# Both attentions of a two-layer decoder: softmax weights turned and copied once in full precision, and multiplied with V head by head onto two halves of the output rows

## The chip, the cores and the metric

The kernel runs on one core of one Trainium2 chip. A core has a matrix engine (TensorE, PE in the rows; its weight loads are listed apart as PEld), a vector engine (VectorE, DVE), a scalar engine (ScalarE, ACT), a general engine (GpSimd, POOL) and DMA queues, issued here by SyncE (SP) and by GpSimd. The metric is the device time of one execution in microseconds (us); lower is better. Every engine runs its own instructions in the order in which the program has them, and waits for the others through semaphores.

## The reference, cut to what matters

Two layers over 1024 tokens with 16 heads of 64 in 4 groups. Layer A ("NSA") has three attention branches per head, over compressed blocks, selected blocks and a window of 256. Each branch is a softmax that is normalised and gated, and the three are added:

```
q, kc, vc, ks, vs, kwn, vwn, gl = split(rmsnorm(x) @ w_in)
p_cmp = softmax(q @ k_cmp.T + bias)              # 63 compressed blocks
p_sel = softmax(q @ ks.T + bias, chosen blocks)  # up to 1024 keys
p_win = softmax(q @ kwn.T + bias, 256 keys)
o = g0 * (p_cmp @ v_cmp) + g1 * (p_sel @ vs) + g2 * (p_win @ vwn)
x = x + o @ w_out ;  x = x + swiglu(rmsnorm(x))
```

Layer B has three dilated windows per head over shared K and V; each gives an output and a log-sum-exp, and the three are merged by their denominators. After it come an output projection, a SwiGLU and a final norm. In both layers the step that matters here is `p @ v`: softmax weights of 128 queries times V of 64 columns, for each head.

## The kernel before, in words

Stages follow each other on the core: projections of layer A, attention A (`cmp_job`, `dense_job`), a dense stage (output projection, SwiGLU, projections for B), attention B (`wide_job`, `near_job`, which share `unit`), and the last dense stage. The instruction order on each engine is fixed when the program is built; the functions below only say what is issued.

An attention job works on 128 queries and a pair of heads (hp is 0 or 1, e is the head within the pair; four heads of a group share one V). Its front makes scores on TensorE (L790 and L791 in A, L1672, L1677 and L1692 in B, always two products each, because queries and keys are held as a high and a low part), adds the bias and takes the extreme on DVE (L793, L1638), and takes the exponential on ACT (L799, L1643); in A POOL scales (L803). Its back, two jobs later, turns the weights `P`, 128 x 128 at a time, on TensorE into a bank `pt` (`transposed`, L328), brings them to SBUF, and multiplies with V into the bank `o`.

The high and low parts are how the kernel gets accuracy out of TensorE's faster product for the type float32r ("fp32r"): `split` makes the high part with an ACT copy (`th`, L165) and the low part with a DVE subtraction (`tl`, L166). A V tile holds 128 columns for each key: 64 of the high part and 64 of the low part. So one product of V (128 columns, as the weight) with 256 columns of turned weights (both heads of a pair for one block of 128 keys) gives 128 output rows, of which the upper 64 must be added to the lower 64. `mm_pv` does this once with `th` (L348) and once with `tl` (L349). Where `whole` is set, one full-precision copy (L332) and one plain float32 product (L347) take their place. For some blocks `copy` is given: ACT or DVE copies (L340), and POOL makes both parts (L341, L342). `evac_o` adds the two halves of the rows: ACT copies one half (L359), DVE adds the other (L360).

In the compressed branch each of the four heads has its own 128-column tile (64 used, 64 zero) in `pc`; four are turned, and two products of 512 columns with `vc` (L760, L761) begin the bank `o`.

Of the kernel before, what the change touches and what calls it, by code (L numbers as in the profile page):

```python
# [10 lines left out]
F32 = mybir.dt.float32  # L11
# [13 lines left out]
G = 4  # L25
# [90 lines left out]
def trunk(ctx, tc, I, out):  # L116
# [206 lines left out]
    def transposed(p, blocks, copy=None, bufs=4, whole=False):  # L323


        ps = bank("pt")
        for i, b in enumerate(blocks):
            nc.tensor.transpose(ps[:, i * 128:(i + 1) * 128], b, ident)  # L328
        w = len(blocks) * 128
        if whole:  # L330
            tf = p.tile([128, 512], F32, name="traw", bufs=2)
            nc.scalar.copy(tf[:, :w], ps[:, :w])  # L332
            return tf, None
# [11 lines left out]
    def mm_pv(o_, v, th, tl, cs, first, last):  # L345
        if tl is None:
            return nc.tensor.matmul(o_, f32(v), th[:, cs], start=first, stop=last, skip_group_check=True)  # L347
        nc.tensor.matmul(o_, v, th[:, cs], start=first, stop=False, skip_group_check=True)  # L348
        return nc.tensor.matmul(o_, v, tl[:, cs], start=False, stop=last, skip_group_check=True)  # L349

    cp_a, cp_v = nc.scalar.copy, nc.vector.tensor_copy

    def evac_o(p, po, dst):

        ov = po[:].rearrange("p (c e q) -> p c e q", e=2, q=128)
        tmp = p.tile([128, 2, 128], F32, name="ot", bufs=2)
        for e in range(2):
            own, oth = slice(64 * e, 64 * e + 64), slice(64 - 64 * e, 128 - 64 * e)
            nc.scalar.activation(tmp[own], ov[oth, :, e, :], AF.Copy)  # L359
            nc.vector.tensor_add(dst[own], ov[own, :, e, :], tmp[own])  # L360
# [20 lines left out]
    vS = dram.tile([2, NT, 128, G, 128], F32, name="vS")  # L381
# [8 lines left out]
    vc = ares.tile([128, G, 128], F32R, name="vc")  # L390
# [4 lines left out]
    with ExitStack() as c:  # L395
# [51 lines left out]
        def evac_v(i):  # L447
            def f(t, ps):
                vt = st.tile([128, G, 128], F32R, name="vt", bufs=2)
# [44 lines left out]
        def compress(i, kc2, weights):  # L494
# [35 lines left out]
            else:  # L530
                for g in range(G):
                    for hd in range(2):
                        nc.tensor.matmul(ps2[0:64, g * 64:(g + 1) * 64], hid[:, hd, g * 64:(g + 1) * 64],
                                         w2t[:, hd, 0, :], start=hd == 0, stop=hd == 1)
                nc.scalar.activation(vc[64:128], kc2[64:128, :, 0:128], AF.Copy, scale=0.0)
                split(vc[0:64, :, 0:64], vc[0:64, :, 64:128], ps2[0:64].rearrange("p (g d) -> p g d", d=64))
# [87 lines left out]
    with ExitStack() as c:  # L624
# [9 lines left out]
        rVs = Ring("V", [128, 4, 128], F32R, [(kA1, 2), (kB, 1)])  # L634
        rVw = [Ring(f"VW{i}", [128, 4, 128], F32R, [((kA0, kA1)[i], 1)]) for i in range(2)]
# [55 lines left out]
        def load_v(i, g, a):  # L691
            t_ = grp["V", i, g, a] = (rVs if i == 0 else rVw[a]).tile()
            nc.sync.dma_start(f32(t_), vS[i, 4 * a:4 * a + 4, :, g, :].rearrange("t p d -> p t d"))

        pcs = [wk.tile([128, 4, 128], F32, name=f"pc{i}") for i in range(2)]
        for pc in pcs:
            nc.gpsimd.memset(pc[:, :, 64:], 0.0)
# [8 lines left out]
        def cmp_job(g, t):  # L706
# [50 lines left out]
            def back():  # L757
                th, tl = transposed(wk, [pc[:, hh, :] for hh in range(4)])
                po = po_[g, t] = bank("o")
                nc.tensor.matmul(po, vc[:, g, :], th, start=True, stop=False, skip_group_check=True)  # L760
                nc.tensor.matmul(po, vc[:, g, :], tl, start=False, stop=False, skip_group_check=True)  # L761
            return back

        def dense_job(g, t, br, hp):
# [41 lines left out]
            def back():  # L806
                po = po_[g, t]
                for b0 in range(0, nb, 2):
                    bs = range(b0, min(b0 + 2, nb))
                    th, tl = transposed(wk, [P[:, e, b * 128:(b + 1) * 128] for b in bs for e in range(2)],  # L810
                                        (cp_a, cp_v)[hp] if br == 2 and b0 == 2 else None,
                                        whole=br == 2 and hp == 1 and b0 == 0)
                    for i, b in enumerate(bs):
                        last = br == 1 and b == nb - 1
                        cs = slice(i * 256, (i + 1) * 256)
                        o_ = po[:, hp * 256:(hp + 1) * 256]
                        v_ = grp["V", br - 1, g, (k0 + b) // 4][:, (k0 + b) % 4, :]
                        mm_pv(o_, v_, th, tl, cs, False, last)
# [1025 lines left out]
```

## Time and profile before

| | us |
|---|---|
| median of 3 runs | 2938.28 (2936.68 to 2944.49) |
| the profiled execution | 2938.84, of which the span from first to last instruction is 2937.1 |
| attention A | 280 to 717 of the span |
| attention B | 1856 to 2178 of the span |
| TensorE busy over the span | 2816.6 (96%) |
| DVE, ACT, POOL busy | 2398.0 (82%), 1621.1 (55%), 1642.7 (56%) |

The busy time of TensorE counts each product from its start to a modelled end, and products overlap at their ends; so what an instruction costs in a stream is the distance from the end of the one before to its own end, which is called its slot below. The granted TensorE clock is 0.989 of full (2.4 GHz) over the span.

### The profile page before, as it was taken

The numbers are of one execution on the slowest core, as the hardware profiler recorded it, in microseconds if no ns is written. First come the engines' busy times: TensorE is split into PE (matmuls) and PEld (weight loads), VectorE is DVE, ScalarE is ACT, GpSimd is POOL, SyncE is SP. The second block draws the span as 40 slices with busy tenths as digits, with TensorE's granted clock in tenths as the row PEclk, the third lists the DMA queues.
The fourth block names the chain that finished last, engine by engine and source line by source line (L and its number), as shares of the span: only waits on it lengthen the run. The fifth ranks groups of instructions, "written<-read, shape, count | busy, mean of one in ns | idle before, by whom it ended". The sixth has DMA issues, their size and how long they took to land. (4 is left out here: it accounts for less than half of the span.)

```text
span 2937.1 us, 44584 instructions
## 1 busy us (share of the span) xinstructions
PE 2816.6 (96%) x14734; PEld 2375.5 (81%) x14734; DVE 2398.0 (82%) x4866; ACT 1621.1 (55%) x3615; POOL 1642.7 (56%) x1727
## 2 busy tenths in 40 slices
PE   9999999999999999999999999899989999999997
PEld 8888888887778888888777778788867788888886
DVE  5543988988888989989976777699998788888887
ACT  5432988887563433334454444699975543343334
POOL 3135766765566556556547777444425655666562
PEclk9999999999999999999999999999999999999999
DMA  8678132112322222231225555865431211112112
GB/s 255 212 240 296 34 105 82 44 47 80 108 62 65 71 73 69 62 85 52 84 85 153 155 162 148 278 201 164 136 136 52 69 57 59 58 47 65 54 44 76
DMA packets 277319, 317.59 MB, mean 108 GB/s; under 512 B 19196, under 2 KB 210733, under 8 KB 277088
## 3 DMA queue, kind: packets, MB, share of 16 engines
q1 hardware_dynamic: 255344, 246.50, 27.8%
q0 software_dynamic: 21744, 68.23, 7.4%
q8 instruction: 117, 1.92, 0.3%
q14 instruction: 114, 0.93, 0.1%
HBM read 243.17 MB, written 87.20 MB: 112 GB/s over the span
## 5 line engine op out<-in xcount | busy, mean ns | idle before, releaser
L885 DVE TENSOR_TENSOR pl<-oT,ph 128x512 fp32r<-128x512 f32 x337 | 350.8, 1058 | 57.5 <-PE dr L934 17.4
L884 ACT ACTIVATE ph<-oT 128x512 fp32r<-128x512 f32 x347 | 210.9, 626 | 203.7 <-PE ux L1082 54.6
L328 PE MATMUL pt<-ident,P 128*128 128x128 f32 x1536 | 243.7, 276 | 11.0 <-DVE tl L166 5.3
L166 DVE TENSOR_TENSOR tl<-pt,th 128x512 fp32r<-128x512 f32 (+1 forms) x336 | 217.5, 653 | 27.2 <-ACT th L165 25.7
L884 ACT ACTIVATE ph<-oTb 128x512 fp32r<-128x512 f32 x239 | 145.6, 627 | 170.4 <-PE ux L1082 52.9
L885 DVE TENSOR_TENSOR pl<-oTb,ph 128x512 fp32r<-128x512 f32 x233 | 213.2, 937 | 28.9 <-PE dr L934 17.4
L939 DVE TENSOR_TENSOR xr<-xr,dr 128x512 f32<-128x512 f32 x320 | 204.0, 679 | 15.9 <-PE dr L934 15.4
L803 POOL TENSOR_SCALAR P<-P,sm,gates 128x384 f32<-128x384 f32 (+7 forms) x256 | 183.4, 728 | 44.8 <-DVE sm L801 39.7
L939 DVE TENSOR_TENSOR xr<-xr,dx 128x512 f32<-128x512 f32 x320 | 204.6, 678 | 1.9 <-PE dx L934 1.9
L165 ACT ACTIVATE th<-pt 128x512 fp32r<-128x512 f32 (+1 forms) x336 | 185.6, 565 | 35.6 <-PE pt L328 31.0
L328 PEld LDWEIGHTS pt<-ident,P 128*128 128x128 f32 x1536 | 178.7, 141 | 32.0 <-DVE tl L166 5.3
L1266 POOL TENSOR_TENSOR oT<-oT,gffn 128x512 f32<-128x512 f32 x92 | 113.5, 1244 | 139.7 <-DMA oT<-in_ffn_w_up_dram 101.8
L799 ACT ACTIVATE P<-P,m 128x384 f32<-128x384 f32 (+7 forms) x256 | 170.7, 669 | 9.0 <-DVE m L797 7.2
L1266 POOL TENSOR_TENSOR oTb<-oTb,gffn 128x512 f32<-128x512 f32 x92 | 109.7, 1199 | 99.6 <-DMA oTb<-in_ffn_w_up_dram 69.1
L349 PE MATMUL o<-tl,V 128*128 128x256 f32 x572 | 159.1, 300 | 6.4 <-POOL tl L342 2.8
L348 PE MATMUL o<-th,V 128*128 128x256 f32 x572 | 159.8, 298 | 3.7 <-DVE o L360 2.2
L341 POOL TENSOR_SCALAR th<-traw 128x256 fp32r<-128x256 f32 x112 | 95.7, 854 | 105.9 <-DVE traw L340 40.2
L1643 ACT ACTIVATE P<-P,st 128x384 f32<-128x384 f32 (+2 forms) x256 | 139.7, 548 | 7.7 <-DVE st L1638 6.4
L1638 DVE CUSTOM_DVE_ANT_0 P<-s,T 128x384 f32<-128x384 f32 (+2 forms) x256 | 114.8, 476 | 12.8 <-PE s L1677 4.6
L349 PEld LDWEIGHTS o<-tl,V 128*128 128x128 f32 x572 | 108.6, 190 | 16.5 <-DVE tl L166 11.0
L348 PEld LDWEIGHTS o<-th,V 128*128 128x128 f32 x572 | 108.9, 190 | 12.4 <-DVE o L360 5.3
L884 ACT ACTIVATE ph<-wd 128x512 fp32r<-128x512 f32 x86 | 53.6, 627 | 99.8 <-PE ux L1082 48.5
(642 smaller groups left out, 9096.1 us busy)
## 6 DMA issues: line engine op xcount, KB each, us to landing
qB<-xr POOLq DMA_DIRECT2D x96, 256.0 KB, 4.6
oT<-in_ffn_w_up_dram SPq DMA_DIRECT2D x92, 256.0 KB, 2.9
oTb<-in_ffn_w_up_dram SPq DMA_DIRECT2D x92, 256.0 KB, 2.9
Q<-qB SPq DMA_DIRECT2D x40, 512.0 KB, 5.8
wd<-in_ffn_w_down_dram SPq DMA_DIRECT2D x66, 256.0 KB, 2.5
oT<-in_b_w_q_dram SPq DMA_DIRECT2D x48, 256.0 KB, 4.5
K<-kBs SPq DMA_DIRECT2D x40, 256.0 KB, 8.6
wraw<-in_a_w_in_dram SPq DMA_DIRECT2D x18, 512.0 KB, 7.4
```

The lines of the kernel that those rows point to most:

```text
L165: prev = nc.scalar.activation(H_, src, AF.Copy)
L166: rest = (eng or nc.vector).tensor_sub(L_, src, f32(H_))
L328: nc.tensor.transpose(ps[:, i * 128:(i + 1) * 128], b, ident)
L348: nc.tensor.matmul(o_, v, th[:, cs], start=first, stop=False, skip_group_check=True)
L349: return nc.tensor.matmul(o_, v, tl[:, cs], start=False, stop=last, skip_group_check=True)
L799: nc.scalar.activation(P[:, e, :n], P[:, e, :n], AF.Exp, bias=mm[:, e:e + 1], scale=-1.0, accum_out=sm[:, e:e + 1])
L803: nc.gpsimd.tensor_scalar(P[:, e, :n], P[:, e, :n], sm[:, e:e + 1], gt(g, t, br, 2 * hp + e, 1), op0=OP.mult, op1=OP.mult)
L884: nc.scalar.activation(h, src, AF.Copy)
L885: (eng or nc.vector).tensor_sub(l, src, f32(h))
L939: nc.vector.tensor_add(xs, xs, banks[t])
L1266: nc.gpsimd.tensor_mul(v, v, gains[:, k:k + 4].unsqueeze(2).to_broadcast([128, 4, 128]))
L1643: nc.scalar.activation(P[:, e, :n], P[:, e, :n], AF.Exp, bias=stats[:, slot, hh:hh + 1], scale=-1.0, accum_out=stats[:, slot, 4 + hh:5 + hh])
```

## The change

The turned weights are copied once to SBUF as float32 (`turned_heads`, tile `pT`), by ACT or by DVE in turn. V and the compressed V are kept as plain float32 with 64 columns for each key. `pv_heads` multiplies V with each head's 128 columns apart: head e of the pair writes output rows 64e to 64e + 63, so that the bank `o` ends with both heads below each other, and one DVE copy takes it to the output. The compressed blocks' weights of two heads (64 + 64 columns) are turned together, against a `vc` that holds V_cmp twice, on the diagonal of a 128 x 128 block. The tiles of V in DRAM and SBUF are half as large.

```diff
-    def transposed(p, blocks, copy=None, bufs=4, whole=False):
-        ...
-        th = p.tile([128, 512], F32R, name="th", bufs=bufs)
-        tl = p.tile([128, 512], F32R, name="tl", bufs=bufs)
-        if copy is None:
-            split(th[:, :w], tl[:, :w], ps[:, :w])
-        else:
-            raw = p.tile([128, 512], F32, name="traw", bufs=2)
-            copy(raw[:, :w], ps[:, :w])
-            nc.gpsimd.tensor_scalar(th[:, :w], raw[:, :w], 1.0, None, op0=OP.mult)
-            nc.gpsimd.tensor_sub(tl[:, :w], raw[:, :w], f32(th[:, :w]))
-        return th, tl
+    def turned_heads(p, blocks, copy):
+        ps = bank("pt")
+        for i, b in enumerate(blocks):
+            nc.tensor.transpose(ps[:, i * 128:(i + 1) * 128], b, ident)
+        w = len(blocks) * 128
+        t = p.tile([128, 512], F32, name="pT", bufs=5)
+        copy(t[:, :w], ps[:, :w])
+        return t
+
+    def pv_heads(po, hp, v, pT, first, last):
+        for e in range(2):
+            prev = nc.tensor.matmul(po[64 * e:64 * e + 64, hp * 128:(hp + 1) * 128], v, pT[:, e * 128:(e + 1) * 128],
+                                    start=first, stop=last, skip_group_check=True)
+        return prev
...
-    vS = dram.tile([2, NT, 128, G, 128], F32, name="vS")
+    vS = dram.tile([2, NT, 128, G, DH], F32, name="vS")
...
-                split(vt[:, :, 0:64], vt[:, :, 64:128], ps[:, :256].rearrange("p (g d) -> p g d", d=64))
-                nc.gpsimd.dma_start(vS[i, t], f32(vt))
+                nc.scalar.copy(vt, ps[:, :256].rearrange("p (g d) -> p g d", d=DH))
+                nc.gpsimd.dma_start(vS[i, t], vt)
...
-                nc.scalar.activation(vc[64:128], kc2[64:128, :, 0:128], AF.Copy, scale=0.0)
-                split(vc[0:64, :, 0:64], vc[0:64, :, 64:128], ps2[0:64].rearrange("p (g d) -> p g d", d=64))
+                nc.gpsimd.memset(vc, 0.0)
+                for u in range(2):
+                    own = slice(64 * u, 64 * u + 64)
+                    for g in range(G):
+                        for hd in range(2):
+                            nc.tensor.matmul(ps2[own, g * 64:(g + 1) * 64], hid[:, hd, g * 64:(g + 1) * 64],
+                                             w2t[:, hd, 0, :], start=hd == 0, stop=hd == 1)
+                    nc.vector.tensor_copy(vc[own, :, own], ps2[own].rearrange("p (g d) -> p g d", d=64))
...
-                th, tl = transposed(wk, [pc[:, hh, :] for hh in range(4)])
+                pT = turned_heads(wk, [pc[:, 2 * c:2 * c + 2, :] for c in range(2)], nc.vector.tensor_copy)
                 po = po_[g, t] = bank("o")
-                nc.tensor.matmul(po, vc[:, g, :], th, start=True, stop=False, skip_group_check=True)
-                nc.tensor.matmul(po, vc[:, g, :], tl, start=False, stop=False, skip_group_check=True)
+                nc.tensor.matmul(po[:, :256], vc[:, g, :], pT[:, :256], start=True, stop=False, skip_group_check=True)
...
+                    copy = (nc.scalar.copy, nc.vector.tensor_copy)[(hp + b0 // 2) % 2]
+                    pT = turned_heads(wk, [P[:, e, b * 128:(b + 1) * 128] for b in bs for e in range(2)], copy)
                     for i, b in enumerate(bs):
-                        mm_pv(o_, v_, th, tl, cs, False, last)
+                        v = grp["V", br - 1, g, (k0 + b) // 4][:, (k0 + b) % 4, :]
+                        pv_heads(po, hp, v, pT[:, i * 256:(i + 1) * 256], False, br == 1 and b == nb - 1)
                 if br == 1 and hp == 1:
-                    evac_o(wk, po, oT[:, 2 * g:2 * g + 2, tok(t)])
+                    nc.vector.tensor_copy(oT[:, 2 * g:2 * g + 2, tok(t)],
+                                          po[:, :256].rearrange("p (c q) -> p c q", q=128))
...
+                    copy = nc.vector.tensor_copy if b0 == 2 or key[1] == 0 and hp == 1 else nc.scalar.copy
+                    pT = turned_heads(wk, [P[:, e, b * 128:(b + 1) * 128] for b in bs for e in range(2)], copy)
                     for i, b in enumerate(bs):
-                            prev = mm_pv(o_, blocks[b], th, tl, cs, b == 0, b == nb - 1)
+                            prev = pv_heads(po, hp, blocks[b], pT[:, i * 256:(i + 1) * 256], b == 0, b == nb - 1)
                 if hp == 1:
-                    evac_o(wk, po, dst)
+                    nc.vector.tensor_copy(dst, po[:, :256].rearrange("p (c q) -> p c q", q=128))
```

Two places on TensorE show what stands in its order. The first is attention A, where the first group reaches its masked tiles (QM is the masked query, K the selected branch's keys, VW and V the window's and the selected branch's V). The names are those of the tiles; the last figures are the output's rows x columns, and x2 or more is a run of equal instructions. Before:

```order
L328 MATMUL pt<-ident,P_3285 128x128 x4
L791 MATMUL s<-K_2739,QM_2786 128x256
L791 MATMUL s<-K_2739,QM_2786 128x512
L791 MATMUL s<-K_2739,QM_2786 128x256
L348 MATMUL o<-th,V_2747 128x256
L349 MATMUL o<-tl,V_2747 128x256
L348 MATMUL o<-th,V_2747 128x256
L349 MATMUL o<-tl,V_2747 128x256
L348 MATMUL o<-th,V_2747 128x256
L328 MATMUL pt<-ident,P_3285 128x128 x2
```

The same place in the changed program, where L327 is the turning, L337 the product with V, L768 and L769 the scores:

```order
L768 MATMUL s<-K_2728,Q_2768 128x512
L337 MATMUL o<-pT,V_2737 64x128 x4
L327 MATMUL pt<-ident,P_3230 128x128 x4
L768 MATMUL s<-K_2728,Q_2770 128x256
L327 MATMUL pt<-ident,P_3230 128x128 x2
L769 MATMUL s<-K_2729,QM_2776 128x256
L769 MATMUL s<-K_2729,QM_2776 128x512
L769 MATMUL s<-K_2729,QM_2776 128x256
L337 MATMUL o<-pT,V_2737 64x128 x2
L327 MATMUL pt<-ident,pc_2681 128x128 x2
L327 MATMUL pt<-ident,P_3323 128x128 x4
```

All products stood at 128 output rows; now runs of two, four or more with 64 output rows stand between products and turnings with 128.

The second place is attention B at a first group's last near jobs (V is the near window's V, cc the merge's coefficients). Before:

```order
L1735 MATMUL pt<-ident,cc 8x128 x4
L1692 MATMUL s<-K_19954,Q_19951 128x256
L1692 MATMUL s<-K_19955,Q_19951 128x256
L328 MATMUL pt<-ident,P 128x128 x3
L1692 MATMUL s<-K_19954,Q_19952 128x256
L1692 MATMUL s<-K_19955,Q_19952 128x256
L348 MATMUL o<-th,V_19956 128x256
L349 MATMUL o<-tl,V_19956 128x256
L348 MATMUL o<-th,V_19956 128x256
L349 MATMUL o<-tl,V_19956 128x256
```

The same place in the changed program:

```order
L337 MATMUL o<-pT,V_19102 64x128 x4
L1706 MATMUL pt<-ident,cc 8x128 x4
L327 MATMUL pt<-ident,P 128x128 x3
L1663 MATMUL s<-K_19100,Q_19099 128x256
L1663 MATMUL s<-K_19101,Q_19099 128x256
L1663 MATMUL s<-K_19100,Q_19096 128x256
L1663 MATMUL s<-K_19101,Q_19096 128x256
L1663 MATMUL s<-K_19100,Q_19097 128x256
L1663 MATMUL s<-K_19101,Q_19097 128x256
L337 MATMUL o<-pT,V_19102 64x128 x4
```

Here, too, each run of products with V is now one of 64 output rows between turnings and scores of 128.

Over the whole program the order has 1,536 products of L337 (912 in attention A, 624 in B), which stand in 229 unbroken runs in A and 162 in B, and 1,600 turnings of L327 where L328 had 1,664.

## Rows read from the trace of the kernel before

**Rows 1.** Busy time by stretch, attention A and attention B. Columns: stretch, its length, then busy us (and instructions) of PE, PEld, DVE, ACT, POOL; the granted TensorE clock, the DMA engines' share, GB/s.
```profile
280.00:717.00 437.00, 416.04 (x2882) 369.89 (x2881) 387.56 (x1589) 380.89 (x1123) 297.40 (x486) 1.00 0.22 63
1856.00:2178.00 322.00, 293.92 (x2163) 262.64 (x2161) 288.92 (x905) 289.32 (x836) 127.38 (x164) 0.99 0.58 177
```

**Rows 2.** TensorE in order of time in the middle of attention A: start us, us from start to end, line, out<-in, rows*columns of the weight, rows x moving columns, count; the slot of one is worked out from ends.
```profile
500.50 0.28 PE L349 MATMUL o<-tl,VW 128*128 128x256 f32 x1
500.62 0.28 PE L348 MATMUL o<-th,VW 128*128 128x256 f32 x1
...
503.97 1.03 PE L347 MATMUL o<-traw,VW 128*128 128x256 f32 x4
504.83 1.04 PE L328 MATMUL pt<-ident,P 128*128 128x128 f32 x8
505.62 0.48 PE L760 MATMUL o<-th,vc 128*128 128x512 f32 x1
505.94 0.40 PE L761 MATMUL o<-tl,vc 128*128 128x512 f32 x1
```

**Rows 3.** Groups of TensorE's instructions in attention A (280 to 717 us): line, out<-in, shapes, count, then busy us, mean ns of one, and the idle time before them with its releasers. L349 and L791 follow their L348 and L790 in the same numbers, L761 its L760.
```profile
L328 PE MATMUL pt<-ident,P 128*128 128x128 f32 x895 | 139.9, 274 | 3.5 <-DVE cd L727 1.2 <-DVE tl L166 1.2 <-ACT QM L754 0.8
...
L348 PE MATMUL o<-th,V 128*128 128x256 f32 x272 | 74.4, 289 | 0.0
L790 PE MATMUL s<-K,Q 128*128 128x512 f32 x96 | 41.7, 436 | 0.3
L790 PE MATMUL s<-KW,Q 128*128 128x384 f32 x96 | 38.0, 396 | 2.8 <-DVE m L793 2.4
L713 PE MATMUL s<-kc,Q 128*128 128x64 f32 x256 | 35.5, 266 | 0.7 <-DVE mp L793 0.2
L348 PE MATMUL o<-th,VW 128*128 128x256 f32 x108 | 33.5, 312 | 0.2 <-POOL th L341 0.2
...
L347 PE MATMUL o<-traw,VW 128*128 128x256 f32 x120 | 31.4, 381 | 0.0
...
L790 PE MATMUL s<-K,Q 128*128 128x256 f32 x64 | 21.6, 345 | 1.6 <-DVE m L793 1.6
L328 PE MATMUL pt<-ident,pc 128*128 128x128 f32 x128 | 19.4, 274 | 0.6 <-POOL pc L736 0.5
L760 PE MATMUL o<-th,vc 128*128 128x512 f32 x32 | 14.2, 444 | 1.0 <-DVE oT L360 0.6 <-ACT th L165 0.4
...
L790 PE MATMUL s<-K,Q 128*128 128x384 f32 x32 | 12.1, 377 | 0.0
L790 PE MATMUL s<-KW,Q 128*128 128x256 f32 x32 | 10.7, 338 | 0.9 <-DVE stl L170 0.6 <-DVE cd L728 0.3
```

**Rows 4.** The same view for attention B (1856 to 2178 us).
```profile
L328 PE MATMUL pt<-ident,P 128*128 128x128 f32 x624 | 101.2, 280 | 7.5 <-DVE tl L166 4.1 <-DVE o L1743 2.0 <-ACT ot L359 0.4
L348 PE MATMUL o<-th,V 128*128 128x256 f32 x284 | 81.1, 307 | 3.7 <-DVE o L360 2.2 <-DVE oTb L360 1.1
...
L1672 PE MATMUL s<-K,Q 128*128 128x256 f32 x256 | 57.0, 305 | 6.0 <-DMA K<-kBs 4.4 <-DVE st L1638 1.4
L1692 PE MATMUL s<-K,Q 128*128 128x256 f32 x256 | 53.0, 314 | 1.6 <-DVE st L1638 1.5
L1677 PE MATMUL s<-K,Q 128*128 128x256 f32 x224 | 44.1, 282 | 2.0 <-DMA K<-kBs 2.0
L347 PE MATMUL o<-traw,V 128*128 128x256 f32 x56 | 14.7, 378 | 0.0
L1742 PE MATMUL pt<-crow,rowsel 128*128 128x512 f32 x31 | 14.0, 476 | 1.6 <-DVE o L1743 1.0 <-DVE crow L166 0.6
```

**Rows 5.** TensorE in order of time where the compression of V ends, in the projections of layer A: L533 is a plain float32 product with a weight of 64 columns onto 64 output rows; L203, L204 and L205 are fp32r products of 512 columns around it.
```profile
203.17 0.40 PE L203 MATMUL mm<-hH,wh 128*128 128x512 f32 x1
203.49 1.03 PE L533 MATMUL cmp<-w2t,hid 128*64 128x64 f32 x14
204.45 0.50 PE L204 MATMUL mm<-hL,wh 128*128 128x512 f32 x1
204.79 0.39 PE L205 MATMUL mm<-hH,wl 128*128 128x512 f32 x1
```

**Rows 6.** The weight loads at the same place; the bracket is idle time before the row and what ended it ("issue": nothing that the profile shows).
```profile
202.34 0.19 PEld L533 LDWEIGHTS cmp<-w2t,hid 128*64 128x64 f32 x2 [0.35 <-issue]
...
203.49 0.89 PEld L533 LDWEIGHTS cmp<-w2t,hid 128*64 128x64 f32 x14 [0.36 <-issue]
```

**Rows 7.** TensorE in order of time around a turning of 16 columns (L753) in attention A.
```profile
330.08 0.34 PE L791 MATMUL s<-KW,Q 128*128 128x384 f32 x1
330.25 0.27 PE L753 MATMUL pt<-ident,mk 128*16 128x128 f32 x1
330.28 0.36 PE L348 MATMUL o<-th,VW 128*128 128x256 f32 x1
```

**Rows 8.** DVE's subtraction and copy of turned weights in attention A (283 to 717 us), in the columns of Rows 3.
```profile
L166 DVE TENSOR_TENSOR tl<-pt,th 128x512 fp32r<-128x512 f32 x182 | 123.5, 684 | 18.4 <-ACT th L165 17.7 <-PE o L348 0.3
...
L340 DVE COPY traw<-pt 128x256 f32<-128x256 f32 x24 | 9.9, 414 | 2.0 <-POOL tl L342 1.8
```

**Rows 9.** Weight loads waiting in attention A (280 to 717 us): engine, what waited, for whom, us in total, times, the longest.
```profile
PEld s L790 <- DVE m L793: 10.6, 23, 1.0
PEld o L349 <- DVE tl L166: 9.6, 27, 0.5
PEld o L349 <- POOL tl L342: 6.5, 11, 1.2
```

More of the change, by code (lines that the diff above doesn't have):

```diff
@@ L389, in trunk @@
     kc = ares.tile([128, G, DH], F32, name="kc")
-    vc = ares.tile([128, G, 128], F32R, name="vc")
+    vc = ares.tile([128, G, 128], F32, name="vc")
     hctx = ExitStack()
@@ L530, in compress @@
             else:
[L531 to L534, printed above, removed]
-                nc.scalar.activation(vc[64:128], kc2[64:128, :, 0:128], AF.Copy, scale=0.0)
-                split(vc[0:64, :, 0:64], vc[0:64, :, 64:128], ps2[0:64].rearrange("p (g d) -> p g d", d=64))
+                nc.gpsimd.memset(vc, 0.0)
[6 more added lines that the diff above has]
+                    nc.vector.tensor_copy(vc[own, :, own], ps2[own].rearrange("p (g d) -> p g d", d=64))
         tok_proj(wv, 304, hT, natural, evac_v(1), range(4, NT))
@@ L633, in trunk @@
         rKw = [Ring(f"KW{i}", [128, (512, 768)[i]], F32R, [((kA0, kA1)[i], 2)]) for i in range(2)]
-        rVs = Ring("V", [128, 4, 128], F32R, [(kA1, 2), (kB, 1)])
-        rVw = [Ring(f"VW{i}", [128, 4, 128], F32R, [((kA0, kA1)[i], 1)]) for i in range(2)]
+        rVs = Ring("V", [128, 4, DH], F32, [(kA1, 2), (kB, 1)])
+        rVw = [Ring(f"VW{i}", [128, 4, DH], F32, [((kA0, kA1)[i], 1)]) for i in range(2)]
         rT = Ring("T", half, F32, [(kA1, 8), (kB, 4)])
@@ L692, in load_v @@
             t_ = grp["V", i, g, a] = (rVs if i == 0 else rVw[a]).tile()
[L693 to L697, printed above, removed]
+            nc.sync.dma_start(t_, vS[i, 4 * a:4 * a + 4, :, g, :].rearrange("t p d -> p t d"))
+        pcs = [wk.tile([128, 4, 64], F32, name=f"pc{i}") for i in range(2)]
         units = [(g, t) for g in range(G) for t in range(NT)]
@@ L1390, in trunk @@
     kBs = dram.tile([3, G, 2, DH, S], F32, name="kBs")
-    vBs = dram.tile([3, NT, 128, G, 128], F32, name="vBs")
+    vBs = dram.tile([3, NT, 128, G, DH], F32, name="vBs")
     second = ("T1", "T2", "T3", "T4", "B22")
@@ L1500, in done @@
                         nc.tensor.transpose(pt[:, s * 128:(s + 1) * 128], cols(got[s, hf]), ident)
-                    vt = vts().bitcast(F32R).rearrange("p (g d) -> p g d", d=128)
-                    split(vt[:, :, 0:64], vt[:, :, 64:128], pt[:, :256].rearrange("p (g d) -> p g d", d=64))
+                    vt = vts()[:, :256]
+                    nc.scalar.copy(vt, pt[:, :256])
+                    vt = vt.rearrange("p (g d) -> p g d", d=DH)
                     if i < 2:
-                        nc.gpsimd.dma_start(vBs[i, t], f32(vt))
+                        nc.gpsimd.dma_start(vBs[i, t], vt)
                     else:
@@ L1570, in trunk @@
         rK = [Ring(f"K{i}", [128, S], F32R, [(bB if i == 0 else bA, 2)]) for i in range(3)]
-        rV = [Ring(f"V{i}", [128, NT, 128], F32R, [(bB if i == 0 else bA, 1)]) for i in range(3)]
+        rV = [Ring(f"V{i}", [128, NT, DH], F32, [(bB if i == 0 else bA, 1)]) for i in range(3)]
         rT0 = Ring("T0", [128, 256], F32, [(bB, 5)])
@@ L1626, in trunk @@
         po_ = {}
-        pick = lambda hp, b0, nb: (cp_a, cp_v)[hp] if nb == 3 and b0 == 2 else None
-        unsplit = lambda key, hp: key[1] == 0 and hp == 1 and key[2] % 2 == 0
         def unit(key, hp, stats, slot, score, bias, n, blocks, dst):
```

35 lines of the change are left out of this document (4 added, 31 removed).

## The prediction

> **What bounds the kernel now.** The busy time by stretch comes first [rows 1]. In attention A, 437 us long, TensorE is busy for 416.04, DVE for 387.56, ACT for 380.89; in attention B, 322 us, they have 293.92, 288.92 and 289.32. Busy TensorE time includes the modelled tails of its products, so it does not say how much room there is. For that I need slots: the distance between the ends of two products that follow each other without a wait.
>
> The order of time gives them [rows 2]. L349 ends at 500.78 and L348 at 500.90: 0.12 us for an fp32r product of 256 columns. L760 ends at 506.10, L761 at 506.34: 0.24 for 512 columns; 384 I put at 0.18. Eight turnings take 1.04, of which one alone takes 0.27 [rows 3]: (1.04 - 0.27) / 7 = 0.11 each. Four plain products L347 take 1.03, one 0.38: 0.217 each. And there are 120 of these in the row where the code issues 60 (15 blocks a group with `whole`, 4 groups, each one call): a plain float32 product runs as two instructions, 0.43 us for 256 columns, against 0.24 for the L348 and L349 that it replaces.
>
> Now the sum for A, with counts of the rows [rows 3], or of the code where a few records are missing: scores 2 x (96 x 0.24 + 128 x 0.18 + 96 x 0.12) = 115; 256 of L713 at 0.11 (weights as wide as a turning's) = 28; 1,040 turnings = 114; 792 products L348 and L349 = 95; L347 120 x 0.217 = 26; L760 and L761 64 x 0.24 = 15. Together 393 of 437: TensorE stands still for about 44. For B [rows 4]: 768 scores x 0.12 = 92; 624 turnings = 69; 568 products = 68; L347 56 x 0.217 = 12; the merge 32 x 0.24 and some 96 small turnings, at most 0.11 each, 18. Together 259 of 322: 63 of standing still. So TensorE does 652 us of work in 759 us of attention. The other engines can give back at most the 107; whatever is added to TensorE's work beyond that must lengthen the kernel.
>
> **What the change takes from TensorE.** 792 + 568 fp32r products (95 + 68), 176 plain ones (26 + 12), the 64 wide products for the compressed branch (15) and 64 of its turnings (7). It adds 32 plain products of 256 columns against `vc`, 64 instructions x 0.217 = 14. What is left without the new products with V is 393 - 95 - 26 - 15 - 7 + 14 = 264 in A and 259 - 68 - 12 = 179 in B, 443 together.
>
> **What it adds: 1,536 products of 64 output rows, 3,072 instructions.** The nearest row is L533: plain float32, a weight of 64 columns, 64 output rows. Its weight loads are 14 in 0.89 and 2 in 0.19 [rows 6], so one each (0.89 - 0.19) / 12 = 0.058 us. That is a floor for any instruction of this shape. L533 moves 64 columns; the new ones move 128, half of the 256 that take 0.217, so 0.109 if each waits for the one before. So the bounds are 0.058 (the two heads' halves of the output run side by side, only the loading of weights counts) and 0.109 (one after another): 1,824 x 0.058 = 106 in A and 1,248 x 0.058 = 72 in B, 178; or 199 + 136 = 335. No row shows two products on different halves, since L533 uses one half only. I take the lower bound, at about 2 to 1: the two heads write different output rows from different columns of the array and share nothing. Side by side, the last instruction of a run has no partner, another 0.05 in each of the 391 runs that the order has, 20 us.
>
> The Trainium skill, TensorE: Matmul & The Clock Gate, Part 3, says that products on different column tiles run concurrently, three of them 2.38 times as fast as in turn; no row here shows it. By that rule a block of 128 keys would take two slots of 0.109 for its four instructions, 768 x 0.218 = 167, an estimate.
>
> **What it adds: a change of shape around every run.** This is where L533 speaks most [rows 5]. L203 ends at 203.57 and L205 at 205.18, 1.61 us. In between lie 14 x 0.058 = 0.81 of L533 and two products of 0.24, 0.48 (L204, L205). 0.32 us are left over, with nothing waited for: the weight load sat idle for 0.36, as it did for 0.35 before the first two [rows 6], and the trace names no releaser. The products around it do not lose time against each other, nor do plain and fp32r ones of full width (L347 follows L349, and L328 follows L347, at their slots [rows 2]). So entering and leaving 64-row products costs about 0.33 us a run: as if the array ran empty and a weight load that is otherwise hidden lay open. The program has 229 runs in A and 162 in B (counted in the order), 229 x 0.33 = 76 and 162 x 0.33 = 53, 129 us.
>
> The Trainium skill, TensorEngine Tiling (Array Packing), Key Properties, says that a change of tiling mode drains TensorE. The trace agrees at L533; it does not at the 16-column turning L753, which ends 0.10 after L791 and lets L348 end 0.12 later [rows 7], both at their slots. So by the page that turning would be dear as well, and by the row it is free. The new products are of L533's kind, no turnings.
>
> **What it takes from the others.** DVE loses its subtractions (182 x 0.684 in A [rows 8]) and gets 92 copies of that width, priced like the subtraction since it reads the same bank, and copies of 256 columns at 0.414. ACT and POOL lose more than they get. None was the bound, none becomes it. What this buys is waits: those of L349 for `tl`, 9.6 and 6.5 us in A [rows 9], have no successor; those for the scores' slots (L790 on DVE, 10.6) and B's first loads (K, 4.4 and 2.0 [rows 4]) stay, if shorter. Bounds for the 107 of standing still: all stays, or all goes. I take half, 53. The evacuation of V and the copies in the projections are hidden: TensorE does not wait for them, and DVE gets less to do there. The halved V loads save bytes, not issues.
>
> **Sum.** TensorE after: 443 + 178 + 20 + 129 = 770, against 652: +118. Standing still 107 - 53: -53. Together +65. The profiled execution took 2938.84 (0.6 above the median of the runs shown, which is nothing here), so 3004. A would go from 437 to about 479, B from 322 to 343.
>
> **Rivals.**
> 1. The halves do not run side by side. Then 443 + 335 + 129 = 907, +255; TensorE is so full that only 30 of standing still remain, -77: +178, 3117. For it: no row shows overlap. Against: different columns, different rows. Chance 0.25.
> 2. The drain does not come, and the halves do overlap: 443 + 178 + 20 = 641, -11; half of the standing still goes, -53: 2875, faster. What decides is the price of a run: at 391 runs, break-even with the sum above is 0.33 - 65 / 391 = 0.16 us. For it: L753 changes width for free [rows 7], and two passages of L533 are few. Against: L533 is the very shape that is added. Chance 0.14.
> 3. The drain is paid where TensorE would have stood still anyway (a run begins when its copy arrives). Half of the 129 hidden gives 3004 - 65 = 2939, no change. For it: runs wait for copies. Against: the order puts other work between turning and product, so that the copy is mostly there. Chance 0.09.
> 4. No drain, but in turn: 443 + 335 = 778, +126 - 53 = +73: 3012. Chance 0.05.
>
> The forecast itself has 0.47. With all the standing still kept it is 3057, with none 2950: its own range.
>
> **Numbers.** 3004. The range reaches from 2940, under all of the forecast, to 3130, above rival 1; rival 2 is left out, and about half of rival 3. About 0.3% (9 us) is what a measurement of this kernel can tell from no change: faster 0.14, same 0.09, slower 0.77.
>
> **What would show it.** L337 in runs of which each begins with an idle weight load of about 0.3 us that no engine ended; starts of the second head's instruction close to the first's (overlap) or 0.109 apart; A near 479 and B near 343 us; DVE below 330 in A. I am wrong if the weight load before a run does not sit idle, or if the spacing within runs is neither 0.058 nor 0.109. The stretches outside the attentions keep their lengths.

## The result, and the profile after

The changed kernel takes **2912.32 us** (2909.76 to 2916.17), the kernel before 2937.98 (2936.68 to 2944.49): a ratio of 0.9909, with a 95% interval of 0.9889 to 0.9929. It is faster by 26 us. The prediction said 3004, slower.

The page's busy times for the span of 2907.8 us:

```profile
PE 2836.9 (98%) x16222; PEld 2317.5 (80%) x16222; DVE 2249.4 (77%) x4603; ACT 1455.7 (50%) x3213; POOL 1458.3 (50%) x1502
```

TensorE is busy for 20 us more than before, in a span that is 29 us shorter. The busy times by stretch, attention A and then attention B (columns as in [rows 1]):

```profile
280.00:717.00 437.00, 435.16 (x3768) 336.04 (x3768) 327.26 (x1485) 294.12 (x923) 222.73 (x388) 1.00 0.20 56
1842.00:2154.00 312.00, 306.57 (x2814) 247.93 (x2813) 229.13 (x800) 221.60 (x652) 28.69 (x38) 0.99 0.59 174
```

In A, TensorE is now busy for 435.16 of 437 us, where it was for 416.04 [rows 1]. DVE, ACT and POOL have lost 60, 87 and 75 us there. The groups of TensorE, in A (four rows) and in B (three), say the same by their last column:

```profile
L327 PE MATMUL pt<-ident,P 128*128 128x128 f32 x912 | 151.3, 283 | 0.0
L337 PE MATMUL o<-pT,V 128*64 128x128 f32 x1152 | 93.2, 284 | 0.0
L337 PE MATMUL o<-pT,VW 128*64 128x128 f32 x672 | 57.9, 288 | 0.0
...
L768 PE MATMUL s<-KW,Q 128*128 128x384 f32 x96 | 38.3, 398 | 0.0
...
L327 PE MATMUL pt<-ident,P 128*128 128x128 f32 x624 | 108.0, 285 | 0.0
L337 PE MATMUL o<-pT,V 128*64 128x128 f32 x1248 | 104.7, 287 | 0.5 <-ACT pT L330 0.4
L1643 PE MATMUL s<-K,Q 128*128 128x256 f32 x256 | 58.1, 308 | 4.8 <-DMA V<-vBs 3.6 <-DVE st L1611 1.2
```

Before the turnings of `P` TensorE stood idle for 3.5 us in A and 7.5 in B [rows 3, 4], and now not at all. The wait of L790 for DVE's extremes (2.4 us in one group of [rows 3]) is gone in the row that answers to it, L768. The largest that is left is one wait in B for a load of V, 3.6 us.

The order of time shows the new products L337 (1,824 in A, 1,248 in B, as predicted) between turnings L327 and scores L768 and L769:

```profile
498.84 0.28 PE L769 MATMUL s<-KW,Q 128*128 128x256 f32 x1
499.05 0.66 PE L337 MATMUL o<-pT,V 128*64 128x128 f32 x8
499.64 0.66 PE L327 MATMUL pt<-ident,P 128*128 128x128 f32 x4
500.23 0.66 PE L337 MATMUL o<-pT,V 128*64 128x128 f32 x8
500.81 0.44 PE L327 MATMUL pt<-ident,P 128*128 128x128 f32 x2
501.19 0.66 PE L337 MATMUL o<-pT,V 128*64 128x128 f32 x8
```

Read the ends, start plus length. Eight L337 end at 499.71, four turnings at 500.30, eight L337 at 500.89, two turnings at 501.25, eight L337 at 501.85. Two turnings fewer shorten their step from 0.59 to 0.36, so a turning costs 0.11 as before; the first of a group costs 0.36 - 0.11 = 0.25, 0.15 more. Eight L337 take 0.59 or 0.60. The first of them, too, ends 0.25 after the instruction before it. If the products ran one after another at 0.109, eight would take 0.87 even without a price at their start. Taken one by one in the trace, the eight end in pairs: the two heads' instructions 0.007 us apart, and each pair 0.109 after the pair before. So the 0.05 an instruction used below is the mean of 0.007 and some 0.10.

The weight loads of the same rows show where that start goes:

```profile
499.05 0.42 PEld L337 LDWEIGHTS o<-pT,V 128*64 128x64 f32 x8
499.63 0.42 PEld L327 LDWEIGHTS pt<-ident,P 128*128 128x128 f32 x4 [0.17 <-issue]
500.23 0.42 PEld L337 LDWEIGHTS o<-pT,V 128*64 128x64 f32 x8 [0.17 <-DVE dg L711]
500.81 0.20 PEld L327 LDWEIGHTS pt<-ident,P 128*128 128x128 f32 x2 [0.17 <-POOL pc L715]
501.18 0.42 PEld L337 LDWEIGHTS o<-pT,V 128*64 128x64 f32 x8 [0.17 <-issue]
501.77 0.31 PEld L327 LDWEIGHTS pt<-ident,P 128*128 128x128 f32 x3 [0.17 <-issue]
```

The load stands idle for 0.17 on every way out of the 391 but one, and for as long on the way in behind a turning. On the way in behind scores the median is 0.14, which the view leaves out, as in the first row. No engine is late: the `dg` and the `pc` that two rows name are tiles of the compressed branch, which these instructions do not read. In and out together come near the 0.36 of L533 [rows 6]; but there all of it lay in front of the products.

### The profile page after: what moved, and what is told of

It reads as the page before. It is cut to its first block, busy times and chain, and to the rows that moved or that the text cites. A ratio compares the mean times of both kernels' runs of the same rounds, so it can differ in the third digit from the quotient of the medians.

```text
span 2907.8 us, 46644 instructions
## 1 busy us (share of the span) xinstructions
PE 2836.9 (98%) x16222; PEld 2317.5 (80%) x16222; DVE 2249.4 (77%) x4603; ACT 1455.7 (50%) x3213; POOL 1458.3 (50%) x1502
## 5 line engine op out<-in xcount | busy, mean ns | idle before, releaser
L327 PE MATMUL pt<-ident,P 128*128 128x128 f32 x1536 | 259.3, 284 | 0.0
L330 DVE COPY pT<-pt 128x256 f32<-128x256 f32 (+1 forms) x264 | 142.6, 541 | 105.0 <-PE pt L327 76.2
L327 PEld LDWEIGHTS pt<-ident,P 128*128 128x128 f32 x1536 | 170.4, 141 | 54.2 <-issue 46.2
L337 PE MATMUL o<-pT,V 128*64 128x128 f32 x2400 | 197.8, 286 | 0.5 <-ACT pT L330 0.4
L330 ACT COPY pT<-pt 128x512 f32<-128x512 f32 (+1 forms) x232 | 123.4, 532 | 118.5 <-PE pt L327 117.3
L337 PEld LDWEIGHTS o<-pT,V 128*64 128x64 f32 x2400 | 125.7, 136 | 52.0 <-issue 19.9
L771 DVE CUSTOM_DVE_ANT_0 P<-s,T 128x128 f32<-128x128 f32 (+3 forms) x192 | 102.2, 549 | 13.3 <-PE s L769 10.6
L909 PE MATMUL dx<-ph 128*128 128x512 f32 x320 | 107.5, 390 | 0.6 <-ACT ph L859 0.6
L909 PE MATMUL dx<-ph,pl 128*128 128x512 f32 x320 | 107.0, 389 | 0.0
L1597 POOL TENSOR_SCALAR_AFFINE_SELECT T<-T 128x256 f32<-128x256 f32 x16 | 6.1, 399 | 196.0 <-DMA T<-sA 104.0
```

What stands on the lines that cost most here:

```text
L330: copy(t[:, :w], ps[:, :w])
L337: prev = nc.tensor.matmul(po[64 * e:64 * e + 64, hp * 128:(hp + 1) * 128], v, pT[:, e * 128:(e + 1) * 128], start=first, stop=last, skip_g ...
L909: nc.tensor.matmul(banks[t], part(a, t)[u], b[v], start=z == 0 and onX != 2, stop=z == 2, skip_group_check=True)
```

## How the runs are counted

For every run the same count was made from its trace, in A and in B; A goes from its first score to its last product with V, which in the kernel before ends at 724 us, not at 717. The slot of each TensorE instruction is the distance between two ends. What a slot has beyond the usual one of its kind (its line, its shape, and whether it begins, continues or leaves a run of 64-row products) is **standing still**; the rest of the stretch is **work**, drains included. A **run** is a row of 64-row products without another instruction between. us throughout.

| kernel | median | A: work + still | B: work + still | runs |
|---|---|---|---|---|
| before | 2937.98 | 390.1 + 53.5 | 258.2 + 64.6 | none |
| changed | 2912.32 | 430.9 + 7.2 | 300.2 + 11.8 | 391 |
| e1_plain_full_width | 2991.56 | 467.1 + 14.6 | 315.4 + 20.8 | none |
| e2_fewer_runs | 2886.93 | 405.8 + 18.2 | 292.2 + 10.1 | 284 |
| e3_dve_load | 2931.26 | 428.2 + 14.7 | 305.0 + 20.1 | 376 |
| e4_pool_chain | 2905.68 | 404.4 + 41.3 | 281.7 + 16.1 | 240 |
| e5_one_half | 3102.68 | 535.7 + 20.4 | 372.4 + 11.6 | 379 |
| e7_old_chain | 2983.59 | 424.1 + 65.1 | 288.5 + 39.5 | 344 |
| e8_turn_all_lag3 | 2898.76 | 405.4 + 21.9 | 294.8 + 14.5 | 283 |

The kernel before had medians of 2939.54 beside e1 to e4, 2933.81 beside e5 to e8 and 2938.44 beside e9 and e10. The second profile of the changed kernel (e10) has 431.0 + 5.5 and 300.2 + 12.9, so the count repeats to about 2 us.

From before to after: work 648 to 731 (+83), standing still 118 to 19 (-99), the rest of the span -13 (-29.3 in all, -16.4 in the attentions). The prediction had +118, -53 and nothing. 2938.84 + 83 - 99 - 13 = 2910, the profiled execution's 2909.95.

## Experiments

**What takes the standing still away?** e1 leaves the kernel before as it is, but turned weights are always copied once and multiplied plain, at full width (128 output rows, no halves), copies by ACT and DVE in turn; the compressed branch and the evacuation of the output stay.

```diff
-            tf = p.tile([128, 512], F32, name="traw", bufs=2)
-            nc.scalar.copy(tf[:, :w], ps[:, :w])
+            tf = p.tile([128, 512], F32, name="traw", bufs=5)
+            turn[0] ^= 1
+            (cp_a, cp_v)[turn[0]](tf[:, :w], ps[:, :w])
...
-                                        whole=br == 2 and hp == 1 and b0 == 0)
+                                        whole=True)
...
-        unsplit = lambda key, hp: key[1] == 0 and hp == 1 and key[2] % 2 == 0
+        unsplit = lambda key, hp: True
```

> The kernel before, in which all turned weights of the window, the selected branch and attention B are copied once (ACT and DVE in turn) and multiplied plain at full width (256 columns, 128 output rows, V as 64 high and 64 low columns); no halves, so no change of shape; the two halves of the rows are still added as before. TensorE's work in the attentions grows by 1,536 x 0.217 - 1,360 x 0.12 - 176 x 0.217 = +132 us. Theory 1 (the standing still goes because one copy takes work and waits off DVE, ACT and POOL, whatever the product's form): it falls from 110 to about 15 as in the changed kernel, 2938 + 132 - 95 = 2975. Theory 2 (in the changed kernel the drains around the runs lie where TensorE would have stood still anyway, and so hide it): without drains the 110 show again, 2938 + 132 = 3070. Half of it, as the prediction had it: 3017.

Measured 2991.56, ratio 1.0178 (1.0163 to 1.0193). Work rose by 134. Standing still fell from 118 to 35, more than the half that the prediction took. The time lies between theory 1 (2975) and the half (3017), nearer to theory 1. TensorE's busy times in A and B (columns as in [rows 1]):

```profile
285.00:766.00 481.00, 476.52 (x2928) 420.42 (x2927) 361.99 (x1517) 329.00 (x1016) 223.95 (x390) 1.00 0.21 58
1904.00:2240.00 336.00, 323.75 (x2173) 290.36 (x2172) 274.01 (x861) 259.36 (x776) 27.95 (x36) 1.00 0.56 169
```

So with the single copy most of the waiting goes also without the halves; but it needs the halves to pay for its dearer products, since at full width the kernel is 52 us slower. e1 alone does not tell the copy from the longer work of TensorE, behind which the other engines have more time; e7 below does.

**What does a run cost?** e2 is the changed kernel, but a job turns all its blocks first and then multiplies them, the last block first, with eight buffers for `pT` rather than five; the same products run in fewer runs.

```diff
...
-                    pT = turned_heads(wk, [P[:, e, b * 128:(b + 1) * 128] for b in bs for e in range(2)], copy)
-                    for i, b in enumerate(bs):
...
-                        pv_heads(po, hp, v, pT[:, i * 256:(i + 1) * 256], False, br == 1 and b == nb - 1)
+                    pTs.append(turned_heads(wk, [P[:, e, b * 128:(b + 1) * 128] for b in bs for e in range(2)], copy))
+                for b in reversed(range(nb)):
...
+                    with after(turned[0] if b == nb - 1 else None):
+                        pv_heads(po, hp, v, pTs[b // 2][:, b % 2 * 256:(b % 2 + 1) * 256], False, br == 1 and b == 0)
```

> The changed kernel, in which a job first turns all its blocks and then multiplies them, last block first, with eight tiles of turned weights instead of five: 284 runs of 64-row products instead of 391, the same products. Theory 1 (TensorE is full, each run costs its 0.30 us): 107 x 0.30 = 32 us less, 2912 - 32 = 2880, less what waiting for a job's last copy brings back (up to 10). Theory 2 (drains lie in standing still): no change, 2905 to 2915.

Measured 2886.93, ratio 0.9824 (0.981 to 0.9839): faster than both kernels. Work is 33 us less for 107 runs less, 0.31 a run. A run of 32 in order of time:

```profile
493.84 0.28 PE L771 MATMUL s<-KW,Q 128*128 128x256 f32 x1
494.05 1.97 PE L339 MATMUL o<-pT,V 128*64 128x128 f32 x32
495.94 1.31 PE L329 MATMUL pt<-ident,P 128*128 128x128 f32 x10
```

From the end at 494.12 to that at 496.02 it takes 1.90: 0.25 for the first, then 31 at 0.053. The ten turnings behind it end 1.23 later: 0.25 and nine at 0.109. So entering and leaving are paid for, and the length of a run adds only its products. Standing still grew by 9 us, most of it before A's scores, which wait 10 us here and 4 in the changed kernel. e8 puts a job's back three jobs behind its front, not two, to win that back.

```diff
-        lag = [2]
+        lag = [3]
...
-        pipelined(jobs(), 2)
+        pipelined(jobs(), 3)
```

> The variant that turns all blocks of a job first and then multiplies, with the back of a job three jobs behind its front rather than two, in both attentions. 283 runs, against 284. Theory (the 18 us of standing still left in A are scores and copies that come just too late): 2870 to 2880. Rival (the buffers of P, four deep, hold the fronts back instead): 2890 to 2920.

Measured 2898.76, ratio 0.988 (0.9864 to 0.9897), behind e2's 0.9824. A keeps its length (427.3 against 424.0), B is 7 us longer (309.3 against 302.3). The time is the rival's, but its reason is not shown: `P` has four buffers in both attentions, A keeps its length, and the loss is B's, whose cause stays open.

**Do the halves overlap?** e5 writes both heads onto the same 64 output rows, side by side in the bank.

```diff
-            prev = nc.tensor.matmul(po[64 * e:64 * e + 64, hp * 128:(hp + 1) * 128], v, pT[:, e * 128:(e + 1) * 128],
-                                    start=first, stop=last, skip_group_check=True)
+            c = hp * 256 + e * 128
+            prev = nc.tensor.matmul(po[0:64, c:c + 128], v, pT[:, e * 128:(e + 1) * 128],
+                                    start=first and e == 0, stop=last, skip_group_check=True)
```

> The changed kernel, but both heads of a pair write the same 64 output rows (0 to 63), each its own 128 columns of the bank, so that no two products can lie on different halves; two DVE copies of 64 rows take the bank out. 379 runs of 64-row products, against 391. Theory (the two heads run side by side in the changed kernel, 167 us for 3,072 instructions): in turn each instruction takes 0.109 us, 335 together, +168; 12 runs less at 0.30, -4; at most the 19 us of standing still are covered: 3060 to 3080. Rival (the spacing comes from the 64-row shape alone, the halves add nothing): 2905 to 2915, spacing 0.05 as before. Between them: if the weight load of 0.058 to 0.07 binds, 2930 to 2960.

Measured 3102.68, ratio 1.0573 (1.0558 to 1.0589). The same eight products, in order of time:

```profile
563.99 0.28 PE L774 MATMUL s<-KW,Q 128*128 128x256 f32 x1
564.20 1.09 PE L338 MATMUL o<-pT,V 128*64 128x128 f32 x8
```

They end 1.02 after L774 (564.27 to 565.29), which is 0.25 + 7 x 0.109; the changed kernel takes 0.59 for them. So in turn each costs 0.109, and on two halves 0.05 in the mean. The time is 23 us beyond the expectation's top. Two things were left out of it. The products of the compressed branch are halved too, 64 instructions more at 0.217, 14 us. And standing still grew from 19 to 32, where a cover of up to 19 had been taken off.

**What had made the waits?** e3 gives DVE back a subtraction beside each ACT copy, whose result nothing reads; e4 sends each tile that ACT copies through a second copy on POOL before the product may read it. The first is load without a chain, the second a chain of two steps, which also loads POOL.

```diff
+        if copy == nc.scalar.copy:
+            j = p.tile([128, 512], F32, name="jl", bufs=1)
+            nc.vector.tensor_sub(j[:, :w], ps[:, :w], t[:, :w])
```

> The changed kernel with a subtraction on DVE beside every copy that ACT makes (it reads the same bank and the copy, and nobody uses what it writes): DVE's work in attention A goes from 327 back to about 415 us of 437, the chain to the products is as short as in the changed kernel; 376 runs. If load on DVE made the standing still of before: 40 to 80 us of it come back, 2945 to 2985. If the length of the chain made it (high part on ACT, then low part on DVE or both on POOL, then the product): no more than 10, 2905 to 2920.

Measured 2931.26, ratio 0.9974 (0.9963 to 0.9986): 19 us more than the changed kernel. Standing still rose by 7.5 in A and 8.3 in B. The time lies between the two theories. The busy times in A (columns as in [rows 1]) show that DVE has the load of the kernel before again, 389 us where that had 388:

```profile
280.00:722.00 442.00, 436.69 (x3770) 338.41 (x3771) 389.46 (x1620) 292.27 (x923) 222.98 (x388) 1.00 0.21 56
```

The subtraction reads the bank `pt`, too, and so keeps it until DVE is done. DVE's load and the bank held for it together bring back 16 of 99.

```diff
-        copy(t[:, :w], ps[:, :w])
+        if copy == nc.scalar.copy:
+            r = p.tile([128, 512], F32, name="rT", bufs=2)
+            copy(r[:, :w], ps[:, :w])
+            nc.gpsimd.tensor_copy(t[:, :w], r[:, :w])
+        else:
+            copy(t[:, :w], ps[:, :w])
```

> The changed kernel in which every copy that ACT makes goes through a second tile and a POOL copy before the product: the chain is about 0.8 us longer for half of the groups, DVE and ACT have the changed kernel's work, POOL goes from 223 to some 330 us of 437 in attention A; the build has 240 runs instead of 391, which takes 151 x 0.30 = 45 us off TensorE. If the chain's length made the standing still: 40 to 80 us come back, 2912 - 45 + 60 = 2927. If DVE's load made it: about 15 stay as they are, 2912 - 45 = 2867, or up to 2885 with POOL's queue.

Measured 2905.68, ratio 0.9891 (0.9874 to 0.9907), between the times of the two theories (2927, and 2867 to 2885). The order changed more than meant: 240 runs, and work 45 us less (151 runs less, 0.30 each, the price of e2 again). In A 34 us of standing still came back, in B 4. The weight loads that wait, in A (columns as in [rows 9]):

```profile
...
PEld s L773 <- DVE mp L776: 11.6, 34, 0.8
...
PEld pt L327 <- ACT rT L332: 5.7, 9, 1.3
...
PEld o L342 <- POOL pT L333: 4.9, 16, 0.9
```

Only 4.9 of it is the product itself waiting for POOL. Turnings wait for a bank that ACT frees late, and scores for DVE. POOL is the engine that scales `P` in A (busy 290.25 there rather than 222.73), and in B it does little; that its queue carries the lateness from tile to tile is argued from this, not shown.

e7 puts all of it together: the changed kernel's products, under the way of copying of the kernel before, engine by engine (ACT copy, then a DVE operation on bank and copy; a copy and two POOL operations where POOL made the parts; one copy where it had one; the output bank by ACT and then DVE).

```diff
...
+        if copy is None:
+            nc.scalar.copy(r[:, :w], ps[:, :w])
+            nc.vector.tensor_tensor(t[:, :w], ps[:, :w], r[:, :w], op=OP.max)
+        else:
+            copy(raw[:, :w], ps[:, :w])
+            nc.gpsimd.tensor_scalar(r[:, :w], raw[:, :w], 0.0, None, op0=OP.mult)
+            nc.gpsimd.tensor_sub(t[:, :w], raw[:, :w], r[:, :w])
...
+            nc.scalar.activation(tmp[own], ov[own], AF.Copy)
+            nc.vector.tensor_tensor(dst[own], ov[own], tmp[own], op=OP.max)
```

> The changed kernel with the whole way of copying of the kernel before, under the new products: where that split, ACT copies the bank and DVE makes the tile that is multiplied out of bank and copy; where POOL made the parts, a copy and two POOL operations; one copy where it had one; the bank of the output goes out by ACT and DVE, two operations for each 64 rows. 344 runs, against 391. Theory (the two-step copies made all of the standing still): A 7 to 54 and B 12 to 65 us of standing still, +99; 47 runs less at 0.30, -14: 2985 to 3005. Rival (half of it came from elsewhere, as the doubled products that each wait twice): standing still 40 to 60 in all, 2925 to 2945.

Measured 2983.59, ratio 1.0166 (1.0151 to 1.0181): 71 us above the changed kernel, and 1 us under the range of the theory. Work fell by 18 (47 runs less), and 86 of the 99 us of standing still are back, 58 in A and 28 in B. The waits in A:

```profile
...
PEld o L359 <- DVE tl L337: 12.4, 30, 1.0
PEld pt L327 <- DVE tl L337: 10.8, 10, 2.5
PEld o L359 <- POOL tl L342: 10.7, 14, 2.9
PEld s L790 <- DVE m L793: 7.5, 19, 1.3
```

These are the names of [rows 9]. Part of the 58 is TensorE's clock. The busy times of A and B, then of four stretches of 4 us in A:

```profile
280.00:768.00 488.00, 456.44 (x3767) 345.48 (x3768) 391.55 (x1595) 373.91 (x1128) 295.26 (x484) 0.97 0.19 51
1896.00:2224.00 328.00, 311.70 (x2789) 249.45 (x2787) 287.79 (x905) 284.92 (x837) 127.36 (x165) 0.98 0.58 166
...
316.00:320.00 4.00, 2.64 (x18) 1.42 (x17) 3.77 (x16) 3.93 (x16) 3.73 (x6) 1.00 0.00 0
320.00:324.00 4.00, 3.52 (x21) 2.24 (x22) 1.84 (x6) 1.43 (x4) 4.00 (x8) 0.54 0.00 0
324.00:328.00 4.00, 4.00 (x24) 2.94 (x24) 3.58 (x15) 1.27 (x3) 0.55 (x2) 0.61 0.01 2
328.00:332.00 4.00, 4.00 (x33) 3.34 (x31) 3.42 (x14) 2.93 (x8) 2.30 (x4) 1.00 0.01 4
```

After TensorE had been busy for 2.64 of 4 us, its granted clock fell near the lower level of 1.2 GHz (0.54 and 0.61 of full) and came back once it was busy throughout. Over A the clock is 0.97, over B 0.98; at most 15 us of A's 488 and 7 of B's 328 can be lost to that. Neither the kernel before nor the changed one falls by more than 0.01 over either stretch. So the old way of copying made most of the standing still, nearly all of A's (43 of 46 even if the clock took the whole 15) and in B 28 of 53 us; and more work on TensorE does not cover it, since TensorE has 64 us more of it here than before. How much is the second step and how much the load is shown for DVE alone, by e3: here ACT and POOL, too, have the load of before again (373.91 and 295.26 in A), and no run gives them that load beside a single copy. The other 25 in B stay open. Some 14 of them are waits of the products with V (18 us before, 4 here). But e1, which keeps the old evacuation of the output there, has 20.8 of standing still, 9 above the changed kernel, so that step alone is not it.

**What of the rest of the program?** e6 puts DVE's subtraction for V's tiles back in the projections (the first diff has the line of B; A's is alike); e9 also the stores of 128 columns a head (second diff, the same for A's `vS`); e10 is the changed kernel beside e9.

```diff
...
+                    nc.vector.tensor_sub(vw[:, 256:], pt[:, :256], vt)
...
```

```diff
-    vBs = dram.tile([3, NT, 128, G, DH], F32, name="vBs")
+    vBs = dram.tile([3, NT, 128, G, 128], F32, name="vBs")
```

> The changed kernel with the DVE subtraction for each V tile in the projections of A and B put back (its result goes to a spare tile; the stores keep their halved size). Theory (the 11 us gained in the two projection stretches are DVE's time at the banks): 2920 to 2925, projection B 7 to 10 us longer. Rival (they come from the halved stores, or from nothing in particular): 2910 to 2914.

> The changed kernel with V's way out of the projections wholly as before: the DVE subtraction, and stores of 128 columns for each head (the loads take the first 64 of them). Theory (the gain outside the attentions is this edit's): 8 to 12 us above the changed kernel on the same chip. Rival (it is the order's, or a spread from one program to the next): within 4 us of it.

> The changed kernel itself, unchanged, on the same chip as the run above, so that a few us can be told: 2908 to 2916.

e6 took 2913.34 (ratio 0.9931, 0.9916 to 0.9946, on a chip where before took 2933.81), e9 2919.34 (0.9937, 0.9923 to 0.9951), e10 2912.08 (0.9906, 0.9893 to 0.992). e9 lies 7.3 us above e10 on one chip, a little under what theory said; the intervals of the two ratios do not meet, but nearly. e6 alone decides nothing: its interval overlaps that of the changed kernel. In the profiles 2.9 of e9's 7.3 come before A and 4.1 between the attentions; e6 has 4 between them as well. Rows that wait for DVE or ACT in projection B, of before, of e9 and of e10:

```profile
PEld ux L1082 <- ACT d L1131: 6.0, 4, 2.2
PEld dx L203 <- DVE xr L1384: 3.5, 1, 3.5
PEld uy L1082 <- ACT d L1131: 3.0, 3, 1.3
...
PEld ux L1059 <- ACT d L1108: 5.3, 5, 1.9
PEld dx L203 <- DVE xr L1361: 3.6, 1, 3.6
PEld uy L1059 <- ACT d L1108: 3.0, 3, 1.2
...
PEld ux L1057 <- ACT d L1106: 3.2, 4, 1.1
PEld dx L203 <- DVE xr L1359: 3.2, 1, 3.2
...
PEld uy L1057 <- ACT d L1106: 1.6, 3, 0.8
```

So some 4 of the 13 us outside the attentions are V's way out of the projections, between the attentions: that stretch is 1129.8 us long in e6 and 1130.1 in e9, 1132.1 in the kernel before, and 1125 to 1128 in the eight profiles that have the new way. The 2.9 before A cannot be counted among the 13: A begins at 280.5 us in the kernel before and at 280.4 in e10. The other 9 have no run that names them; about half of these lie behind B (758 us before, 754 in the changed kernel), where e9 loses nothing (751, as e10).

## Why the prediction was wrong

**The reading of the bound was right.** TensorE's 652 of work before were 648 by the count, its standing still 107 were 118 (A was cut off 7 us before its end), and TensorE now stands still for 19 of 750 us of attention. DVE in A has 327, as said (below 330).

**The drain was right in size.** 0.33 a run was predicted from two passages of L533 [rows 5, 6]; it is 0.30 in e4 and 0.31 in e2, and it splits into 0.14 going in and 0.15 or more coming out. 391 x 0.30 = 117 against 129, -12. Its place was not quite as said: the idle load in front of a run is 0.17 or less, not about 0.3, and as much lies behind it. The Trainium skill, TensorEngine Tiling (Array Packing), Key Properties, has such a drain for every change of tiling, and the runs of 64-row products agree (0.30 each). As before [rows 7], the 16-column turning keeps its 0.11 between full-width products in the changed kernel as well; whether it is a change of tiling, no run here shows.

**The overlap was right in kind, and mis-sized.** The floor of 0.058, the spacing of L533's weight loads, was no floor: 64-column loads for the two halves go side by side too (eight take 0.42 above). e5 has 0.109 for 128 columns in turn, which would be 0.055 for L533's 64; so 0.058 was more likely the price of its columns than of its loads, which no run tests. The mean over a run is 0.048 to 0.054, 167 in all, where floor and unpaired ends had 178 + 20: -31. The estimate by the rule of the Trainium skill, TensorE: Matmul & The Clock Gate, Part 3 (two slots of 0.109 for four instructions) was also 167, and the trace agrees: a pair every 0.109.

**The step that failed is the half.** "Bounds for the 107 of standing still: all stays, or all goes. I take half, 53." It was 99 of 118. The prediction counted as gone the products' waits that name `tl` [rows 9], 16 us, and as staying, if shorter, those of the scores. But by the count the scores' waits in A fell from 15.3 to 3.5, the turnings' from 9.8 to 1.5 and, in B, from 18.1 to 0.7; the wait of L348 in B, which names the old evacuation, from 12.1 to at most 1.3. Of all these only the turnings' name a low part, and only in part. In A that is this row (columns as in [rows 9]); for B, [rows 4] has 4.1:

```profile
PEld pt L328 <- DVE tl L166: 3.3, 8, 0.9
```

The prediction did not count these two, but with them, too, the waits that name `tl` are less than a third of the 99 that went. e7 shows that the old way of copying stood behind nearly all of A's, and e1 agrees. e3 shows that DVE's freed time, even with the bank's, is the smaller part. How the one wait makes the others is argued, not shown: while a tile waits for its second engine, the bank `pt`, DVE's next extreme and the next job's scores are late as well. The row of a wait told who came last, not what had made it late.

**Outside the attentions "hidden" is shown wrong by some 4 us** (e6, e9), of 13 by which the program got shorter there. TensorE waits in projection B for ACT and DVE, and those rows were there to be read; the prediction looked only at whether TensorE waits for V's copies themselves.

The miss from +65 to -29 is 94: 46 from the half, 35 from TensorE's work (31 overlap, 12 drain, less 8 that the sum had not), 13 from outside. With all the standing still gone the prediction's own bound was 2950; no choice of that one term would have given 2912. Rivals 2 (2875) and 3 (2939) gave nearer times for reasons that did not come. Against rival 2, drains cost 117 us. Against rival 3, they do not lie in standing still: in e2 and e4 each run less took its full 0.30 off TensorE's work.

## What to carry to other kernels

Where the bounding engine stands still, find the chain that makes each wait late, not the engine that the wait names; here a change that took a step out of it removed 99 of 118 us, where half had been guessed. So price the engine's own work, and test how much hangs on the chain by putting the step back alone. 64-row products on two halves run at twice the rate of one half, and each run of them costs 0.30 us, for entering and leaving together: so gather them into long runs, which here is worth another 25 us (2886.93) at the price of some 9 us of waiting.

## What the runs showed of the hardware beyond that

Plain float32 products of 128 columns on alternate halves of the output end in pairs, 0.007 us apart within a pair and 0.109 from pair to pair, weight loads included; on one half each takes 0.109 (e5). Leaving 64-row products for full-width work leaves the weight load idle for 0.17, and entering them for 0.14 to 0.17 in the median; a turning of 16 columns costs no slot more [rows 7]. And waits can cost a second time: where e7's TensorE was busy for 2.64 of 4 us, the next 8 us ran at a granted clock of 0.54 and 0.61.
